# Closing block of a Winograd-form MLP product: three steps by token tile instead of two, two more sets of weight tiles, and the outputs' vector operations in another written order

## The chip, the cores and the metric

The kernel runs on one core of a Trainium2 chip. The metric is the time of one execution in device microseconds (us); a kernel's time is the median of its timed runs. The profile comes from one further execution with the hardware profiler. TensorE (PE) multiplies matrices, VectorE (DVE), ScalarE (ACT) and GpSimd (POOL) do the elementwise work, and SyncE (SP) issues the transfers (DMA).

## The reference, cut to what matters

One decoder layer for 512 tokens of width 1024 in fp32: a gated mixer of attention and convolution, then a squared-ReLU MLP, each with an RMSNorm before and after it. The change lies in the last part, the product with `w_ff2` and what follows it:

```python
f = jnp.square(jax.nn.relu(rms_norm(x, g_pre) @ w_ff1)) @ w_ff2   # (512 x 4096) @ (4096 x 1024)
x = x + rms_norm(f, g_post)          # x + f * rsqrt(mean(f*f) + eps) * g_post
```

## The kernel before, in words

**Precision.** Each fp32 operand is split in two parts, `hi` (a rounded copy, written by ScalarE) and `lo` (the rest, a subtraction on VectorE: lines 729 and 730 in `split`). `mm3` (lines 89 to 91) makes one product out of three matmuls: hi by hi, hi by lo, lo by hi. All matmuls of the stage concerned have 512 columns.

**The second MLP product** takes 16 steps `p`, each over 256 of the 4096 hidden units. A step is a 2 by 2 block product (two halves of the tokens, two halves of the 1024 columns), done in the Winograd form with seven products instead of eight. Three of the seven are summed over all steps in a first sweep, which runs together with the first MLP product. Then follows the second sweep, in which the change lies: four products `n` = 0 to 3 for two token tiles `t` = 0, 1. Each of the eight pairs (n, t) has a PSUM bank of its own, `bcc[n][t]`, that sums over p. A step of the second sweep is therefore 4 x 2 x 3 = 24 matmuls.

**Operands of a step** (`second_operands`). Four transfers of 256 KB bring quarters of `w_ff2`: one goes to tag `whi`, three to tag `raw`, which has six buffers, enough for two steps. The stationary operand `l` (split of `f1[p]`, 128x1024) has four buffers. The moving operand is a pair of weight tiles, `yh` and `yl`, each with four slices n. Tag `sw` has four buffers, that is two sets, so the split of step p into its weight tiles has to wait until the matmuls of step p - 2 have read theirs. Slice 1 is the split of a difference `t1` (line 774), the others are splits of the transferred quarters.

**Closing block.** Steps 1 to 13 go one after the other. The last TAIL = 2 steps are taken together: for t = 0 and then 1, for n = 0 to 3, the products of both steps are made, and thereby bank (n, t) is complete. What is left is VectorE's: combine the banks with the sums `e`, `g`, `h` of the first sweep into output tiles `o_[t + 2]` (from n = 0 and 1) and `o_[t]` (from n = 2 and 3), each in two column halves. `post` then takes the squares on ScalarE (line 650), the scale of the rows on GpSimd (`v_o`, line 652, and `r_o`, line 148), multiplies each half by the gain in place (line 834), and `finish` multiplies by the row scale, adds the residual `x1` (line 827) and issues the output transfer (line 828). The multiplication in place may only start when ScalarE has read the half. One of the additions to `e` is on GpSimd (line 852).

**Order of the queues.** The framework's scheduler settles each engine's order at compile time: by the order in the program, among the instructions that its own timing takes to be ready. On the chip every queue runs in that order. So the written order isn't always the order of the queue.

Of the kernel before, what the change touches and what calls it, by code (L numbers as in the profile page):

```python
# [12 lines left out]
F32R = mybir.dt.float32r  # L13
BF16 = mybir.dt.bfloat16
I32 = mybir.dt.int32
AF = mybir.ActivationFunctionType
ALU = mybir.AluOpType
# [33 lines left out]
LOOK = 2  # L51
BRIDGE = 4
SPLIT = 2 * P
TAIL = 2
LN0, LN1, LN2 = 0, 2, 3


# [1 line left out]
def decoder_block(ctx: ExitStack, tc: tile.TileContext, a: dict, out: bass.AP):  # L59
# [18 lines left out]
    def stile(name, dt=F32):  # L78
        return spool.tile([P, 512], dt, tag="s", name=name, bufs=6)

    def junk(name, n):
        return spool.tile([P, 1024], BF16, tag="s", name=name, bufs=6)[:, :n]
# [14 lines left out]
    def rtile(name, n=512):  # L97
        return stage.tile([P, 512], F32, tag="raw", name=f"raw_{name}", bufs=NRAW)[:, :n]
# [28 lines left out]
    def stat(name, n=1, tag="stat", bufs=8):  # L127
        return const.tile([P, n], F32, tag=tag, name=name, bufs=bufs)
# [17 lines left out]
    def rstd_of(v, name, n=1):  # L146
        r = stat(name, n)
        pool.tensor_tensor(r, v, mhalf if n == 1 else mhalf.broadcast_to([P, n]), ALU.pow)
        return r
# [57 lines left out]
    with ExitStack() as s1:  # L207
# [89 lines left out]
        def products(t, ab):  # L297
            for k in range(KD):
                zmm(t, k, ab)
# [220 lines left out]
    def wtile(name, dt=F32):  # L520
        return r3.tile([P, 2, 512], dt, tag="w", name=name, bufs=14)
# [124 lines left out]
    def square_sums(src, name, jk=None):  # L646

        ss = stat(f"ss_{name}", 2)
        for hf in range(2):
            act.activation(junk(f"j_{name}{hf}", 512) if jk is None else jk[:, hf, :], src[hf], AF.Square, scale=1.0 / 32.0, accum_out=ss[:, hf:hf + 1])  # L650
        v = stat(f"v_{name}")
        pool.tensor_scalar(v, ss[:, 0:1], ss[:, 1:2], EPS, ALU.add, ALU.add)
        return rstd_of(v, f"r_{name}")
# [74 lines left out]
    def split(hi, lo, src):  # L728
        act.copy(hi, src)  # L729
        dve.tensor_tensor(lo, src, f32(hi), ALU.subtract)  # L730
# [29 lines left out]
    def first_sweep(p, ops):  # L760
        left, w = ops
        for n, (bank, l) in enumerate(zip(acc, left)):
            products(bank, l, [x[:, n, :] for x in w], p == 0, p == NP - 1)

    def second_operands(p):

        b12, b11, b21, b22 = (quarter(2 * p + r, c, *t) for r, c, *t in (
            (0, 1, "whi", NSPLIT), (0, 0), (1, 0), (1, 1)))
        t1 = stage.tile([P, 512], F32, tag="wlo", name=f"t1{p}", bufs=NSPLIT)
        l = htile(f"l{p}")  # L770
        w = [r3.tile([P, 4, 512], F32R, tag="sw", name=f"y{x}{p}", bufs=4) for x in "hl"]
        split(l[:, 0:2, :], l[:, 2:4, :], f1[p])
        split(w[0][:, 0, :], w[1][:, 0, :], b11)
        dve.tensor_tensor(t1, b12, b11, ALU.subtract)
        for n, src in ((1, t1), (2, b21), (3, b22)):
            split(w[0][:, n, :], w[1][:, n, :], src)
        return l, w


# [2 lines left out]
    def second_products(p, ops, which, toks=(0, 1)):  # L782
        l, w = ops
        for n in which:
            r, c = LEFT[n]
            products(bcc[n], [l[:, r, half[c]], l[:, 2 + r, half[c]]], [x[:, n, :] for x in w], p == 0, p == NP - 1, toks)

    ops = {}
    for p in range(NP):
# [29 lines left out]
        second_products(p, second_operands(p), range(4))  # L819

    o_ = [wtile(f"o{t}") for t in range(NT)]

    def finish(t, r):
        for c, n in ((0, 512), (512, 512)) if t != 1 else ((0, 512), (512, 256), (768, 256)):
            hf, c1 = divmod(c, 512)
            piece = o_[t][:, hf, c1:c1 + n]
            dve.scalar_tensor_tensor(piece, piece, r, x1[t][hf][:, c1:c1 + n], ALU.mult, ALU.add)  # L827
            sp.dma_start(out[t * P:(t + 1) * P, c:c + n], piece)

    def post(t):  # L830
        src = [o_[t][:, hf, :] for hf in range(2)]
        r = square_sums(src, f"o{t}")
        for hf in range(2):
            dve.tensor_tensor(src[hf], src[hf], gout[:, hf * 512:(hf + 1) * 512], ALU.mult)  # L834
        finish(t, r)

    last = [(p, second_operands(p)) for p in range(NP - TAIL, NP)]
    for t in range(2):
        v = stile(f"v{t}")
        for n in (0, 1, 2, 3):  # L840
            for p, x in last:
                second_products(p, x, (n,), (t,))
            bank = bcc[n][t]
            if n == 0:
                act.copy(v, bank)
                dve.tensor_tensor(o_[t + 2][:, 0, :], v, h[:, t, :], ALU.add)
            elif n == 1:
                dve.tensor_tensor(g[:, t, :], g[:, t, :], bank, ALU.add)
                dve.tensor_tensor(e[:, t, :], e[:, t, :], bank, ALU.add)  # L849
                dve.tensor_tensor(o_[t + 2][:, 1, :], g[:, t, :], v, ALU.add)  # L850
                post(t + 2)
                pool.tensor_tensor(e[:, t, :], e[:, t, :], v, ALU.add)  # L852
            elif n == 2:
                dve.tensor_tensor(o_[t][:, 0, :], v, bank, ALU.add)
            else:
                dve.tensor_tensor(o_[t][:, 1, :], e[:, t, :], bank, ALU.add)
                post(t)


def _layout(i):  # L860
# [58 lines left out]
```

## Time and profile before

| what | value |
|---|---|
| median of 3 runs | 820.9 us (820.53 to 821.85) |
| profiled execution: its time | 821.58 us |
| its span, first to last instruction | 819.8 us |
| TensorE busy | 789.4 us, 96% of the span |
| VectorE busy | 631.7 us, 77% |
| mean granted TensorE clock | 0.985 of full |

The profiled execution took 1.78 us more than its span and 0.68 us more than the median. Times of single instructions are counted from the start of the span. A matmul's start-to-start distance in the stage concerned is 0.227 us; its shown duration of 0.39 us overlaps the next one.

### The profile page before, as it was taken

The page shows a single profiled execution, that of the slowest core. Times are in us where ns is not written, and L with a number is a line of the kernel's source. Part 1 is how long each engine was busy: PE and PEld are TensorE (multiplying, and loading weights), DVE is VectorE, ACT ScalarE, POOL GpSimd, SP SyncE. Part 2 cuts the span into 40 slices and gives each one's busy share as a digit, 9 for nine tenths or more (in the row PEclk, how much of TensorE's full clock was granted, in tenths as well). Part 3 has the DMA queues.
Part 4 walks back from the last instruction along what each step waited for, and adds up shares of the span by engine and source line. Part 5 has one row for each costly group of instructions (what it writes and reads, how often), then busy time and mean ns, then how long its engine had stood idle before and what let it go on. Part 6 is the DMA issues. An engine that isn't in the chain of part 4 may idle for free. (4 is left out here: it accounts for less than half of the span.)

```text
span 819.8 us, 11002 instructions
## 1 busy us (share of the span) xinstructions
PE 789.4 (96%) x3786; PEld 662.7 (81%) x3786; DVE 631.7 (77%) x1046; ACT 419.7 (51%) x792; POOL 215.6 (26%) x203
## 2 busy tenths in 40 slices
PE   8989999999999999899999999999999999999991
PEld 8977888888887888687877898888888888788881
DVE  5689999999999996587563538676766666798777
ACT  7566876876763323366442314444444344556642
POOL 4244334333534545647640110000000000000003
PEclk9999999999999999899999999999999999999996
DMA  8412121122112223235551014444433434565422
GB/s 269 137 42 91 52 81 53 45 88 71 65 65 90 97 97 113 93 134 171 172 191 39 17 36 154 142 167 142 162 133 129 155 128 146 179 214 204 167 69 102
DMA packets 54344, 96.36 MB, mean 118 GB/s; under 512 B 6288, under 2 KB 11280, under 8 KB 54288
## 3 DMA queue, kind: packets, MB, share of 16 engines
q1 hardware_dynamic: 53856, 94.09, 34.3%
q0 software_dynamic: 432, 1.57, 0.6%
q8 instruction: 30, 0.49, 0.3%
q14 instruction: 26, 0.21, 0.1%
HBM read 93.54 MB, written 2.10 MB: 117 GB/s over the span
## 5 line engine op out<-in xcount | busy, mean ns | idle before, releaser
L562 DVE SCALAR_TENSOR_TENSOR cv<-u,convw,cv 128x512 f32<-128x512 f32 x232 | 161.9, 747 | 0.2
L90 PE MATMUL pf<-h2l,whi_f 128*128 128x512 f32 (+1 forms) x256 | 96.2, 376 | 0.0
L89 PE MATMUL pf<-h2h,whi_f 128*128 128x512 f32 (+1 forms) x256 | 96.2, 376 | 0.0
L91 PE MATMUL pf<-h2h,wlo_f 128*128 128x512 f32 (+1 forms) x256 | 96.0, 376 | 0.0
L115 DVE TENSOR_TENSOR wlo_f<-raw_f,whi_f 128x512 fp32r<-128x512 f32 x60 | 41.1, 691 | 61.1 <-ACT whi_f L114 58.8
L852 POOL TENSOR_TENSOR e<-e,v 128x512 f32<-128x512 f32 x2 | 3.2, 1594 | 321.5 <-DVE e L849 321.5
L114 ACT CAST whi_f<-raw_f 128x512 fp32r<-128x512 f32 x60 | 36.9, 621 | 81.4 <-DMA raw_f<-in_w_ff 42.7
L115 POOL TENSOR_TENSOR wlo_gt<-raw_gt,whi_gt 128x512 fp32r<-128x512 f32 x32 | 43.9, 1373 | 50.5 <-ACT whi_gt L114 50.5
L89 PEld LDWEIGHTS pf<-h2h,whi_f 128*128 128x128 f32 x256 | 48.2, 188 | 8.8
L90 PEld LDWEIGHTS pf<-h2l,whi_f 128*128 128x128 f32 x256 | 48.2, 188 | 8.7
L91 PEld LDWEIGHTS pf<-h2h,wlo_f 128*128 128x128 f32 x256 | 48.2, 188 | 8.7
L89 PE MATMUL pg<-hTh,whi_gt 128*128 128x512 f32 x128 | 51.9, 405 | 0.0
L90 PE MATMUL pg<-hTl,whi_gt 128*128 128x512 f32 x128 | 50.8, 397 | 0.0
L91 PE MATMUL pg<-hTh,wlo_gt 128*128 128x512 f32 x128 | 50.7, 396 | 0.0
L89 PE MATMUL p<-yh,l 128*128 128x512 f32 x128 | 49.7, 390 | 0.0
L90 PE MATMUL p<-yl,l 128*128 128x512 f32 x128 | 49.7, 389 | 0.0
L91 PE MATMUL p<-yh,l 128*128 128x512 f32 x128 | 49.5, 389 | 0.0
L729 ACT CAST yh<-f 128x512 fp32r<-128x512 f32 x48 | 28.1, 619 | 32.8 <-PE p L90 25.2
L730 DVE TENSOR_TENSOR yl<-f,yh 128x512 fp32r<-128x512 f32 x48 | 31.7, 686 | 12.9 <-ACT yh L729 12.9
L114 ACT CAST whi_gt<-raw_gt 128x512 fp32r<-128x512 f32 x32 | 19.8, 618 | 41.3 <-PE pg L90 38.4
L729 ACT CAST xh<-t 128x512 fp32r<-128x512 f32 x48 | 29.8, 621 | 19.5 <-DVE t L754 19.5
L730 DVE TENSOR_TENSOR xl<-t,xh 128x512 fp32r<-128x512 f32 x48 | 31.6, 686 | 0.0
(314 smaller groups left out, 2279.8 us busy)
## 6 DMA issues: line engine op xcount, KB each, us to landing
f<-in_w_ff SPq DMA_DIRECT2D x128, 256.0 KB, 3.0
raw_f<-in_w_ff SPq DMA_DIRECT2D x64, 256.0 KB, 3.1
raw_gt<-in_w_zm SPq DMA_DIRECT2D x32, 256.0 KB, 2.5
raw_gb<-in_w_zm SPq DMA_DIRECT2D x16, 256.0 KB, 2.6
raw_ga<-in_w_zm SPq DMA_DIRECT2D x16, 256.0 KB, 2.6
raw_wo<-in_w_o SPq DMA_DIRECT2D x16, 256.0 KB, 2.6
raw_pw<-in_w_pw SPq DMA_DIRECT2D x16, 256.0 KB, 2.9
raw_wout<-in_w_out SPq DMA_DIRECT2D x16, 256.0 KB, 2.7
```

The source lines that it names most:

```text
L89: pe.matmul(o, lhsT=lh, rhs=rh, start=first, stop=False)
L90: pe.matmul(o, lhsT=lh, rhs=rl, start=False, stop=False)
L91: return pe.matmul(o, lhsT=ll, rhs=rh, start=False, stop=last)
L114: recent[act] = act.copy(hi, raw)
L115: recent[e] = e.tensor_tensor(lo, raw, f32(hi), ALU.subtract)
L562: dve.scalar_tensor_tensor(co[j] if tap == CW - 1 else acc[j], src, convw[:, i, tap:tap + 1], acc[j], ALU.mult, ALU.add)
L729: act.copy(hi, src)
L730: dve.tensor_tensor(lo, src, f32(hi), ALU.subtract)
L852: pool.tensor_tensor(e[:, t, :], e[:, t, :], v, ALU.add)
```

## The change

The closing block takes three steps together instead of two (p = 13, 14, 15). Two further sets of weight tiles come from the pool of tag `w`, whose tiles for the first MLP product's results are free by then: steps 6, 9 and 12 use set 0 and step 14 uses set 1; the other steps go on alternating over the two sets of tag `sw`. So the last three steps have three sets.

In the closing block the operations on the outputs are written in another order. A half of an output tile is now added up, squared and at once multiplied by the gain into a tile of its own (tag `raw`), no longer in place; the row scale is asked for after the second half, and `finish` of an output tile is written one or two banks later. The sum `u` = bank 1 + `v` serves both `o_[t + 2]` and `e`; with that, GpSimd's addition to `e` goes, and the additions of a bank to `g` and to `e` become additions of `u`. VectorE has 29 operations on the outputs on either side.

```diff
-TAIL = 2
+TAIL = 3
+THIRD = {6: 0, 9: 0, 12: 0, 14: 1}
...
+    spare = {}
+
+    def right_tiles(p):
+
+
+        if p in THIRD:
+            n = THIRD[p]
+            if n not in spare:
+                spare[n] = [[wtile(f"y{x}{n}{i}", F32R) for i in range(2)] for x in "hl"]
+            return [(lambda i, v=v: v[i // 2][:, i % 2, :]) for v in spare[n]]
+        return [(lambda i, v=v: v[:, i, :]) for v in (r3.tile([P, 4, 512], F32R, tag="sw", name=f"y{x}{p}", bufs=4) for x in "hl")]
+
...
-        w = [r3.tile([P, 4, 512], F32R, tag="sw", name=f"y{x}{p}", bufs=4) for x in "hl"]
+        w = right_tiles(p)
         split(l[:, 0:2, :], l[:, 2:4, :], f1[p])
-        split(w[0][:, 0, :], w[1][:, 0, :], b11)
+        split(w[0](0), w[1](0), b11)
         dve.tensor_tensor(t1, b12, b11, ALU.subtract)
         for n, src in ((1, t1), (2, b21), (3, b22)):
-            split(w[0][:, n, :], w[1][:, n, :], src)
+            split(w[0](n), w[1](n), src)
         return l, w
...
     o_ = [wtile(f"o{t}") for t in range(NT)]
+    scaled, ss_ = {}, [stat(f"ss_o{t}", 2) for t in range(NT)]
+
+    def half_row(t, hf, x, y):
+
+        o = o_[t][:, hf, :]
+        dve.tensor_tensor(o, x, y, ALU.add)
+        act.activation(junk(f"j_o{t}{hf}", 512), o, AF.Square, scale=1.0 / 32.0, accum_out=ss_[t][:, hf:hf + 1])
+        scaled[t, hf] = rtile(f"og{t}{hf}")
+        dve.tensor_tensor(scaled[t, hf], o, gout[:, hf * 512:(hf + 1) * 512], ALU.mult)
+
+    def scale_of(t):
+        v = stat(f"v_o{t}")
+        pool.tensor_scalar(v, ss_[t][:, 0:1], ss_[t][:, 1:2], EPS, ALU.add, ALU.add)
+        return rstd_of(v, f"r_o{t}")
 
     def finish(t, r):
         for c, n in ((0, 512), (512, 512)) if t != 1 else ((0, 512), (512, 256), (768, 256)):
             hf, c1 = divmod(c, 512)
-            piece = o_[t][:, hf, c1:c1 + n]
+            piece = scaled[t, hf][:, c1:c1 + n]
             dve.scalar_tensor_tensor(piece, piece, r, x1[t][hf][:, c1:c1 + n], ALU.mult, ALU.add)
             sp.dma_start(out[t * P:(t + 1) * P, c:c + n], piece)
 
-    def post(t):
-        src = [o_[t][:, hf, :] for hf in range(2)]
-        r = square_sums(src, f"o{t}")
-        for hf in range(2):
-            dve.tensor_tensor(src[hf], src[hf], gout[:, hf * 512:(hf + 1) * 512], ALU.mult)
-        finish(t, r)
-
     last = [(p, second_operands(p)) for p in range(NP - TAIL, NP)]
+    scales = {}
     for t in range(2):
-        v = stile(f"v{t}")
+        v, u = stile(f"v{t}"), stile(f"u{t}")
         for n in (0, 1, 2, 3):
             for p, x in last:
                 second_products(p, x, (n,), (t,))
             bank = bcc[n][t]
             if n == 0:
                 act.copy(v, bank)
-                dve.tensor_tensor(o_[t + 2][:, 0, :], v, h[:, t, :], ALU.add)
+                half_row(t + 2, 0, bank, h[:, t, :])
+                if t:
+                    finish(0, scales[0])
             elif n == 1:
-                dve.tensor_tensor(g[:, t, :], g[:, t, :], bank, ALU.add)
-                dve.tensor_tensor(e[:, t, :], e[:, t, :], bank, ALU.add)
-                dve.tensor_tensor(o_[t + 2][:, 1, :], g[:, t, :], v, ALU.add)
-                post(t + 2)
-                pool.tensor_tensor(e[:, t, :], e[:, t, :], v, ALU.add)
+                dve.tensor_tensor(u, bank, v, ALU.add)
+                half_row(t + 2, 1, u, g[:, t, :])
+                scales[t + 2] = scale_of(t + 2)
+                dve.tensor_tensor(e[:, t, :], e[:, t, :], u, ALU.add)
             elif n == 2:
-                dve.tensor_tensor(o_[t][:, 0, :], v, bank, ALU.add)
+                half_row(t, 0, bank, v)
+                finish(t + 2, scales[t + 2])
             else:
-                dve.tensor_tensor(o_[t][:, 1, :], e[:, t, :], bank, ALU.add)
-                post(t)
+                half_row(t, 1, bank, e[:, t, :])
+                scales[t] = scale_of(t)
+    finish(1, scales[1])
```

## Rows read from the trace of the kernel before

**Rows 1.** Page, part 1: busy us, share of the span and instructions of each engine.

```profile
PE 789.4 (96%) x3786; PEld 662.7 (81%) x3786; DVE 631.7 (77%) x1046; ACT 419.7 (51%) x792; POOL 215.6 (26%) x203
```

**Rows 2.** Busy time by stretch: length, each engine (instructions), granted clock, DMA share, GB/s.

```profile
738.50:776.00 37.50, 37.50 (x167) 31.07 (x166) 30.60 (x43) 21.44 (x35) 0.00 (x0) 1.00 0.57 196
...
795.20:803.30 8.10, 8.10 (x36) 6.39 (x35) 8.10 (x13) 2.94 (x9) 2.80 (x3) 1.00 0.15 59
803.30:819.80 16.50, 0.04 (x1) 0.00 (x0) 11.85 (x18) 3.32 (x9) 5.40 (x7) 0.58 0.26 99
```

**Rows 3.** Chain that ended last, in order of time: start us, us, what.

```profile
791.86 0.24 PE p L90
...
792.12 0.63 ACT yh L729
...
816.30 0.40 DVE o L827
```

**Rows 4.** Timeline of PE: start us, duration us, engine, line, operation, out<-in, form, count.

```profile
786.71 0.39 PE L89 MATMUL p<-yh,l 128*128 128x512 f32 x1
...
802.95 0.39 PE L91 MATMUL p<-yh,l 128*128 128x512 f32 x1
```

**Rows 5.** Timeline of ACT; in brackets the idle time before and its releaser.

```profile
792.12 0.62 ACT L729 CAST yh<-f 128x512 fp32r<-128x512 f32 x1 [3.25 <-PE p L90]
...
812.86 0.63 ACT L650 ACTIVATE j_o<-o 128x512 bf16<-128x512 f32 x1 [1.80 <-DVE o L856]
813.39 0.19 ACT L650 ACTIVATION_READ_ACCUMULATOR j_o<-o 128x1 f32 x1
```

**Rows 6.** Timeline of DVE, one step of the second sweep (12, up to 13).

```profile
776.46 0.69 DVE L730 TENSOR_TENSOR yl<-f,yh 128x512 fp32r<-128x512 f32 x1 [1.10 <-ACT yh L729]
...
778.97 1.23 DVE L730 TENSOR_TENSOR l<-f,l 128x1024 fp32r<-128x1024 f32 x1
780.12 0.69 DVE L774 TENSOR_TENSOR t<-f,f 128x512 f32<-128x512 f32 x1
781.90 0.69 DVE L730 TENSOR_TENSOR yl<-f,yh 128x512 fp32r<-128x512 f32 x1 [1.10 <-ACT yh L729]
```

**Rows 7.** Timeline of DVE, from the last step's splits to the end.

```profile
792.78 0.69 DVE L730 TENSOR_TENSOR yl<-f,yh 128x512 fp32r<-128x512 f32 x1 [2.94 <-ACT yh L729]
...
795.19 0.68 DVE L846 TENSOR_TENSOR o<-v,h 128x512 f32<-128x512 f32 x1
...
797.59 1.79 DVE L834 TENSOR_TENSOR o<-o,g_out 128x512 f32<-128x512 f32 x1
799.30 0.68 DVE L854 TENSOR_TENSOR o<-v,p 128x512 f32<-128x512 f32 x1
799.90 0.68 DVE L834 TENSOR_TENSOR o<-o,g_out 128x512 f32<-128x512 f32 x1
800.50 1.40 DVE L827 SCALAR_TENSOR_TENSOR o<-o,r_o,x 128x512 f32<-128x512 f32 x2
...
812.09 0.67 DVE L856 TENSOR_TENSOR o<-e,p 128x512 f32<-128x512 f32 x1
...
815.15 1.54 DVE L827 SCALAR_TENSOR_TENSOR o<-o,r_o,x 128x512 f32<-128x512 f32 x3 [0.85 <-POOL r_o L148]
```

**Rows 8.** Timeline of POOL in the closing block.

```profile
797.22 1.61 POOL L852 TENSOR_TENSOR e<-e,v 128x512 f32<-128x512 f32 x1 [318.75 <-DVE e L849]
...
799.63 0.56 POOL L148 TENSOR_TENSOR r_o<-v_o,mhalf 128x1 f32<-128x1 f32 x1
...
813.68 0.80 POOL L652 TENSOR_SCALAR v_o<-ss_o 128x1 f32<-128x1 f32 x1 [3.22 <-ACT j_o L650]
```

**Rows 9.** Line 725, quarters of `w_ff2` issued between 738 and 785 us.

```profile
DMA to landing us min/median/max: 2.5/3.0/4.7
```

**Rows 10.** Busy time by stretch, columns as in the second group; the clock is third last.

```profile
710.00:715.00 5.00, 4.13 (x19) 3.12 (x18) 5.00 (x9) 4.99 (x9) 0.00 (x0) 1.00 0.65 213
...
806.00:807.00 1.00, 0.00 (x0) 0.00 (x0) 1.00 (x3) 0.13 (x1) 0.00 (x0) 0.50 0.64 250
```

More of the change, by code (lines that the diff above doesn't have):

```diff
@@ L785, in second_products @@
             r, c = LEFT[n]
-            products(bcc[n], [l[:, r, half[c]], l[:, 2 + r, half[c]]], [x[:, n, :] for x in w], p == 0, p == NP - 1, toks)
+            products(bcc[n], [l[:, r, half[c]], l[:, 2 + r, half[c]]], [x(n) for x in w], p == 0, p == NP - 1, toks)
     ops = {}
```

## Prediction

> **What bounds the kernel now.** I start from the busy shares: TensorE is busy for 96% of the span [rows 1], so a change can only win in what little is left. The busy times by stretch say where that is. From 738.5 to 776 us TensorE is busy without a gap, and it still is from 795.2 to 803.3, but in the last 16.5 us it has no work, while VectorE is busy for 11.85 of them [rows 2]. The chain of waits says since when VectorE sets the end: TensorE is in the chain up to 792.1 us; there ScalarE's rounding of the last step's weights (`yh`) follows, and from then on VectorE's instructions, broken by short pieces of ScalarE and GpSimd, up to 816.7 [rows 3]. What ScalarE waited for at 792.12 was TensorE [rows 5]: step 15 fills the set of weight tiles that step 13 has just finished reading. VectorE comes to step 15's first `yl` at 792.78, having idled 2.94 us, and to the first output operation at 795.19 [rows 7]. By then TensorE has only 8 us of matmuls left; the six banks still open close within them, and VectorE falls behind: it comes to the last addition at 812.09. From that addition on, a fixed chain runs: squares on ScalarE at 812.86, the row scale on GpSimd from 813.68, the last three output pieces at 815.15 [rows 5, 7, 8], and the transfer until 819.8. That is 819.8 - 812.09 = 7.71 us, of which 3.06 lie between the addition and the first piece.
>
> TensorE's own end can hardly move. The last 72 matmuls (three steps) start at 786.71, and the last one starts at 802.95 [rows 4]: 16.24 us for 71 distances, 0.229 each, while full rate here is 0.2267 (a step of 24 takes 5.44 us, as the distance of 776.46 and 781.90 in [rows 6] also says). So at most 0.15 us is lost there. The gain has to come out of the 16.5 us behind TensorE.
>
> **The change part by part.**
>
> *Three steps in the closing block.* The same 72 matmuls, in another order: a bank now closes every 9 matmuls, 2.04 us, beginning at 786.71 + 2.04 + about 0.2 for the matmul's own length = 788.96, and the eighth at 803.24. Before, a bank closed every 1.36 us from 793.6 on. VectorE's output work can start some 6 us earlier, if its operands are done by then.
>
> *Are the operands there in time?* The closing block needs the first slice of step 15 six matmuls after 786.71: `yh` at 788.07, `yl` at 788.30. Before, `yl` was ready at 792.78 + 0.69 = 793.47. So 5.17 us have to be won, just under one step, and that is what the further sets permit: with three sets in turn from step 6 on, a step's split waits for the step three back, 5.44 us earlier. VectorE must also be quick enough. One step holds it for 5.44 us, of which it waits 1.10 [rows 6]; without the wait 4.34. The transfers allow about the same: a `raw` buffer is free after a step's first `yl` (0.69), the next quarter lands 3.0 later [rows 9], `t1` (0.60) follows: 4.3. So each step from 6 on gains up to 1.1 us, and after five steps, by step 11, the lead of one step is full. Step 13's first `yl` then starts at 781.90 - 5.44 = 776.46. Step 14 has a set of its own and follows at 780.8; step 15 at 785.2, first `yl` ready at 785.9. In the worse order, in which step 15's `l` (its buffer is free when step 11's matmuls end, 792.12 - 2 x 5.44 = 781.24) stands ahead of step 14's splits, step 14 starts at 781.24 + 1.23 for ScalarE's part (taken as long as VectorE's of the same 1024 columns, 778.97) + 1.15 for VectorE's + 0.60 for `t1` = 784.2 and step 15 at 786.6, ready at 787.3. Both are ahead of 788.30, by 2.4 and 1.0 us. The cost for TensorE is zero, hidden by this margin; without it each microsecond late costs one. VectorE is done with the operands between 787.6 and 789.0.
>
> *The output operations.* Their number on VectorE doesn't change, 29. Each of the simple ones takes 0.60 us start to start (four from 795.19 to 797.59), two pieces of `finish` 1.40 [rows 7]. GpSimd's additions to `e` go, and something more goes with them: the multiplication at 797.59 took 1.79 us, where that at 799.90 took 0.68, and GpSimd's addition ran from 797.22 to 798.83 [rows 7, 8]. The second token tile shows the same pattern, so VectorE gets back twice 1.1 us. Multiplying into a separate tile removes the wait for ScalarE's squares; before, the scheduler had put the next bank's addition (line 854, 799.30) in that place, so this gives order and little time. The scaled halves take `raw` buffers that no transfer needs any more; the two that come round again were sent out more than 7 us before.
>
> *Sum, bank by bank* (start of the first operation; bank closing in brackets), VectorE at 0.60 and 1.40: t = 0: n0 788.96 (788.96), n1 791.0 (791.0), four operations to 793.4; n2 793.4 (793.0), half a row and `finish(2)` to 796.0; n3 796.0 (795.1) to 797.2. t = 1: n0 797.2 (797.1) to 798.4; `finish(0)` waits for its scale, 796.0 + 3.06 = 799.06, to 800.46; n1 800.46 (799.2) to 802.86; n2 802.86 (801.2) to 804.06; `finish(3)` at its scale, 801.06 + 3.06 = 804.12, to 805.52; n3, the last addition, at 805.52 (803.2). Before, it was at 812.09. Gain 6.57 us. With the 7.71 us behind it the span is 813.2, and the profiled execution 821.58 - 6.6 = 815.0; it had stood 0.68 above the median, so I take the median's 820.9 - 6.6 = **814.3 us**.
>
> *Bounds.* The last addition can't come before bank (3, 1) closes: 803.24, a gain of 8.85, 812.05 us. From the other side, no lead at all: 5.17 us of the gain are lost, 819.5 us.
>
> **The rivals.**
>
> *1. Another queue order, faster.* The written order puts `finish(3)` ahead of the last addition. The scheduler has reordered here before (line 854 stands between two of line 834 [rows 7]). If it draws the last addition ahead, that starts at 804.06, and `finish(3)` lies in the shadow of the last scale: gain 8.0, 812.9 us. For it speaks that the scale comes only at 804.1; against it, that VectorE would idle only 0.06 us in the written order.
>
> *2. VectorE held up by GpSimd's small operations.* The 1.79 us of [rows 7] show that a multiplication can wait for GpSimd. Four pairs of small operations remain, some 0.56 and 0.80 long [rows 8]. If each pair held VectorE for 0.56 us, 2.2 us would be lost: 816.5. Against it stands the multiplication at 799.90, which took 0.68 although GpSimd's `r_o` ran from 799.63 to 800.19. The Trainium skill, "SBUF — State Buffer", section "Who interferes with whom", says that a VectorE instruction with two SBUF inputs and a GpSimd instruction that reads SBUF exclude each other for a whole instruction. For the large addition the trace agrees (1.79 us); for the 128x1 operations the row at 799.90 does not.
>
> *3. No lead, no change.* If the steps from 6 on gain nothing (VectorE's queue held by a `t1` whose quarter lands late, say), step 15 comes at 792.78 as now; TensorE stands still for 5.17 us in the middle of the closing block, and all banks close that much later: 819.5 us. Against it stand the 1.10 us of waiting in each step that would have to persist though its cause is gone.
>
> *4. No lead, and a lower clock: slower.* The place is the same pause at 788 us. After TensorE's end the granted clock is 0.50 at 806 us, the lower of its two levels (1.2 instead of 2.4 GHz), 2.7 us after the last matmul's end; a pause of 0.87 us within 710 to 715 left it at 1.00 [rows 10]. A pause of 5 us could thus leave some of the 66 remaining matmuls at half rate, 0.227 us more each, at most 15 us: 819.5 to 834.5. It is slower than before from the seventh such matmul on, measurably (0.2%, 1.6 us, about what a measurement of this kernel can tell from no change) from the fourteenth. The Trainium skill, "TensorE: Matmul & The Clock Gate", section "HAM oscillation — how this bites in real kernels", says that pauses for data throttle the clock and that work then goes on slowly at first; no row here shows matmuls after such a pause.
>
> **How the numbers follow.** Forecast 0.66, rival 1 0.14, rival 2 0.05, rival 3 0.10, rival 4 0.05. In rival 3 a partly built lead is as likely as none; it ends between 814.3 and 819.5, so of its 0.10 I give 0.03 to faster and 0.07 to same. Faster: 0.66 + 0.14 + 0.05 + 0.03 = 0.88; same 0.07; slower 0.05. The range goes from the bound of the early side, 812.0, over rivals 1 and 2 to 817.5, which also takes in a lead that is short by 3 us; outside it are what is left of rival 3 and rival 4. The likeliest case alone: 813 to 816.
>
> **What would show it.** In the profile after: step 13's first `yl` near 776.5 and step 15's before 788.3; TensorE without a pause up to 803; the first output operation near 789; no VectorE multiplication above 0.8 us; the last addition near 805.5; some 10 us from TensorE's end to the end of the span instead of 16.5. The prediction is wrong if TensorE pauses around 788, if the queue of VectorE holds output operations ahead of step 15's splits, or if the last addition comes later than 808.

## The result, and the profile after

The change makes the kernel faster: 816.46 us (median of 4 runs, 814.52 to 817.37) beside 820.71 us for the kernel before (4 runs, 820.40 to 821.85), a ratio of 0.9931 with the interval 0.9908 to 0.9954. The gain is 4.25 us, where 6.6 were forecast; 816.46 lies inside the range of 812.0 to 817.5, but just outside the 813 to 816 that the prediction gave for its likeliest case. The profiled execution took 816.91 us with a span of 815.1 us, where the prediction's sum gave 815.0 and 813.2.

The page's busy shares (columns as in [rows 1]) hardly move:

```profile
PE 791.0 (97%) x3786; PEld 664.7 (82%) x3786; DVE 627.9 (77%) x1046; ACT 420.3 (52%) x792; POOL 211.7 (26%) x201
```

The stretches do, which is why the stretch and not the share is to be read. Busy time by stretch of the kernel after, columns as in [rows 2]:

```profile
738.50:776.00 37.50, 37.50 (x168) 31.03 (x167) 34.47 (x50) 25.35 (x40) 0.00 (x0) 1.00 0.68 221
796.20:804.20 8.00, 8.00 (x36) 6.35 (x34) 6.82 (x12) 2.16 (x6) 0.86 (x2) 1.00 0.35 133
804.20:815.10 10.90, 0.06 (x1) 0.00 (x0) 6.38 (x11) 1.93 (x6) 1.94 (x4) 0.67 0.26 96
```

In the first stretch VectorE now works 34.47 us instead of 30.60: it waits less for a set of weight tiles and runs ahead. In the last one it has 11 instructions left instead of 18, and that stretch is 10.9 us long instead of 16.5. TensorE has its full clock up to its end and no pause in the closing block: in its timeline the first of the 72 matmuls and the last are

```profile
787.78 0.39 PE L90 MATMUL p<-yh,l 128*128 128x512 f32 x1
...
803.87 0.39 PE L92 MATMUL p<-yh,l 128*128 128x512 f32 x1
```

16.09 us for 71 distances, 0.2267 each. VectorE's timeline of the kernel after (start, duration, engine, line, operation, out<-in, form, count; in brackets the idle time before and its releaser), as [rows 6, 7] for before:

```profile
766.65 0.69 DVE L731 TENSOR_TENSOR yl<-f,yh 128x512 fp32r<-128x512 f32 x1 [1.10 <-ACT yh L730]
...
782.97 0.69 DVE L731 TENSOR_TENSOR yl<-f,yh 128x512 fp32r<-128x512 f32 x1 [0.74 <-ACT yh L730]
...
790.64 0.69 DVE L840 TENSOR_TENSOR o<-p,h 128x512 f32<-128x512 f32 x1 [3.69 <-ACT v L866]
791.37 0.69 DVE L843 TENSOR_TENSOR raw_og<-o,g_out 128x512 f32<-128x512 f32 x1
792.06 0.69 DVE L871 TENSOR_TENSOR u<-p,v 128x512 f32<-128x512 f32 x1
792.78 0.69 DVE L840 TENSOR_TENSOR o<-u,g 128x512 f32<-128x512 f32 x1
...
795.53 0.75 DVE L854 SCALAR_TENSOR_TENSOR raw_og<-raw_og,r_o,x 128x512 f32<-128x512 f32 x1 [0.25 <-POOL r_o L149]
...
798.18 0.69 DVE L843 TENSOR_TENSOR raw_og<-o,g_out 128x512 f32<-128x512 f32 x1
799.98 0.75 DVE L854 SCALAR_TENSOR_TENSOR raw_og<-raw_og,r_o,x 128x512 f32<-128x512 f32 x1 [1.11 <-POOL r_o L149]
800.65 0.69 DVE L840 TENSOR_TENSOR o<-p,h 128x512 f32<-128x512 f32 x1
...
805.98 0.75 DVE L854 SCALAR_TENSOR_TENSOR raw_og<-raw_og,r_o,x 128x512 f32<-128x512 f32 x1 [0.25 <-POOL r_o L149]
...
807.91 0.68 DVE L840 TENSOR_TENSOR o<-p,e 128x512 f32<-128x512 f32 x1
...
810.49 1.54 DVE L854 SCALAR_TENSOR_TENSOR raw_og<-raw_og,r_o,x 128x512 f32<-128x512 f32 x3 [1.17 <-POOL r_o L149]
```

Step 11's first `yl` is at 766.65 us. The operands of step 15 start at 782.97, the output operations at 790.64, after 3.69 us in which VectorE has nothing to do. The last addition is at 807.91, the last pieces end at 810.49 + 1.54 = 812.03.

**How to compare the kernels.** The start of the closing block (its first matmul) differs by some microseconds from profile to profile, by what happens upstream (run e11 shows one part of it). So each kernel is read from there on, with three numbers: S, from the block's first matmul (with two steps: from the first of the last 72, where step 13 begins) to VectorE's first output operation; L, from that operation to the end of VectorE's last pieces; T, from the start of the last matmul to the end of the span. All come from the timelines. Before: S = 795.19 - 786.71 = 8.48, L = 816.69 - 795.19 = 21.50, T = 819.8 - 802.95 = 16.86 (span 819.81). After: S = 2.86, L = 21.39, T = 11.27. In the table, T - S - L is -13.1 with two steps and -13.0 with three (the block's 16.2 or 16.1 us less 3.1 for the last transfer), so T differs between kernels only by S and L. This is partly arithmetic; what the traces add is that the 72 matmuls take 16.1 to 16.2 us and the last transfer 3.1 in every kernel of the table. S is mainly what the block changes, L mainly what the operations and their order change.

| kernel | S | L | T | ratio to before (95%) |
|---|---|---|---|---|
| before | 8.48 | 21.50 | 16.86 | 1 |
| after | 2.86 | 21.39 | 11.27 | 0.9931 (0.9908 to 0.9954) |
| e1: block alone | 2.86 | 23.79 | 13.68 | 0.9954 (0.9939 to 0.9970) |
| e2: operations alone | 8.48 | 22.13 | 17.47 | 1.0021 (1.0006 to 1.0036) |
| e3: a set for step 14 only | 3.14 | 21.76 | 11.89 | 0.9935 (0.9920 to 0.9949) |
| e4: after, queue as written | 2.86 | 20.77 | 10.66 | 0.9938 (0.9919 to 0.9956) |
| e5: after, additions first | 2.25 | 20.43 | 9.70 | 0.9900 (0.9885 to 0.9915) |
| e7: before, addition on VectorE | 8.49 | 22.72 | 18.09 | 1.0019 (1.0006 to 1.0033) |
| e8: two steps, queue of e5 | 8.48 | 20.33 | 15.69 | 0.9985 (0.9968 to 1.0001) |
| e9: e5, splits put back | 2.24 | 20.13 | 9.38 | 0.9905 (0.9889 to 0.9920) |
| e10: before, splits put back | 8.49 | 21.50 | 16.86 | 0.9988 (0.9975 to 1.0001) |
| e11: after, once more | 2.85 | 21.38 | 11.26 | 0.9939 (0.9916 to 0.9963) |

Each ratio is to runs of the kernel before on the same chip; e6 was run once and stands below.

### The profile page after: what moved, and what is told of

It is laid out like the page before. It is cut to its first block, busy times and chain, and to the rows that moved or that the text cites. A ratio compares the mean times of both kernels' runs of the same rounds, so it can differ in the third digit from the quotient of the medians.

```text
span 815.1 us, 10990 instructions
## 1 busy us (share of the span) xinstructions
PE 791.0 (97%) x3786; PEld 664.7 (82%) x3786; DVE 627.9 (77%) x1046; ACT 420.3 (52%) x792; POOL 211.7 (26%) x201
## 3 DMA queue, kind: packets, MB, share of 16 engines
q0 software_dynamic: 432, 1.57, 0.6%
```

## The experiments

### e1 and e2: the change's two halves

e1 has the three-step block and its sets with the output operations of before (below, against before). e2 is the reverse: the kernel after with these lines taken back.

```diff
-TAIL = 2
+TAIL = 3
+THIRD = {6: 0, 9: 0, 12: 0, 14: 1}
...
-        w = [r3.tile([P, 4, 512], F32R, tag="sw", name=f"y{x}{p}", bufs=4) for x in "hl"]
+        w = right_tiles(p)
```

> The three-step closing block and its weight tiles, with the output operations as they were before (gain multiplied in place, one addition to e on GpSimd). Measure: the stretch from the start of the last matmul to the end of the span, 16.85 us before the change and 11.23 us with the whole change. Theory 1, the block is the main cause: banks close every 2.04 us and VectorE keeps up, so most of the gain is there, stretch about 12.5 us, some 4.4 us faster than before. Theory 2, the order of the output operations is the main cause and VectorE is the bound in any case: the stretch stays above 15 us, gain under 2 us.

> The new output operations alone, with the closing block of two steps and two sets of weight tiles. Theory 1 (block is the main cause): VectorE still begins its output work only after step 15's splits, at 795.2 us, and is the bound from there; it gets back the two waits of 1.1 us at GpSimd's addition and some idle time, stretch from the last matmul's start to the end about 14.5 us, gain about 2.3 us. Theory 2 (order is the main cause): stretch below 12.5 us, gain above 4 us. Theory 3 (order is worth nothing): 16.8 us, no change.

e1: 818.67 us (5 runs; before 822.14, 14 runs). e2: 823.41 us (10 runs). The block alone brings T from 16.86 to 13.68, the operations alone cost 0.6, and both together bring 5.6: the halves don't add up. S shows the block's part whole, 5.62 us in e1 as in the change; e1 loses 2.29 of it in L. VectorE's timeline of e1:

```profile
790.80 0.69 DVE L859 TENSOR_TENSOR o<-v,h 128x512 f32<-128x512 f32 x1 [3.69 <-ACT v L858]
...
795.62 0.91 DVE L847 TENSOR_TENSOR o<-o,g_out 128x512 f32<-128x512 f32 x1 [0.19 <-ACT j_o L651]
...
809.99 0.68 DVE L869 TENSOR_TENSOR o<-e,p 128x512 f32<-128x512 f32 x1
...
813.05 1.54 DVE L840 SCALAR_TENSOR_TENSOR o<-o,r_o,x 128x512 f32<-128x512 f32 x3 [0.84 <-POOL r_o L149]
```

In e1 VectorE has eight idle times of 0.19 to 0.85 in the stretch, 4.84 us in all: four for the row scale, 3.36 us, and four for ScalarE's squares, 1.48 us, which must have read a half before the multiplication in place may start; the same operations in the kernel before wait three times, 1.55 us. In e2 the new operations wait for the scale four times:

```profile
801.23 1.41 DVE L841 SCALAR_TENSOR_TENSOR raw_og<-raw_og,r_o,x 128x512 f32<-128x512 f32 x2 [0.76 <-POOL r_o L148]
...
805.07 0.75 DVE L841 SCALAR_TENSOR_TENSOR raw_og<-raw_og,r_o,x 128x512 f32<-128x512 f32 x1 [1.10 <-POOL r_o L148]
...
812.13 1.42 DVE L841 SCALAR_TENSOR_TENSOR raw_og<-raw_og,r_o,x 128x512 f32<-128x512 f32 x2 [0.84 <-POOL r_o L148]
813.46 0.68 DVE L827 TENSOR_TENSOR o<-p,e 128x512 f32<-128x512 f32 x1
...
816.04 1.54 DVE L841 SCALAR_TENSOR_TENSOR raw_og<-raw_og,r_o,x 128x512 f32<-128x512 f32 x3 [1.16 <-POOL r_o L148]
```

That is 3.86 us in the four waits. Late banks aren't the reason (and behind the last of the four no addition is left): the last matmul of e2 starts at 803.21, so at 812.13 every bank is long complete, and yet the last addition stands behind these pieces, at 813.46. e8 below puts the additions ahead and has an L of 20.33 instead of 22.13. The prediction counted 2.2 us for GpSimd's hold alone, and e2's expectation 2.3 us of gain for the operations; without the block, and in the scheduler's order, they are worth nothing.

### e3: is the lead built from step 6 on needed?

```diff
-THIRD = {6: 0, 9: 0, 12: 0, 14: 1}
+THIRD = {14: 0}
```

> The change without set 0 (steps 6, 9 and 12 go back to the two alternating sets); only step 14 has a set of its own, so no step before 14 can get a lead. Theory A, a set for step 14 is enough: step 15 then takes the set of step 12, which is free when the closing block begins, its first yl is ready about 1.4 us later, just when the seventh matmul wants it: TensorE pauses 0.3 us at most, the stretch from the last matmul to the end stays within 0.7 us of 11.2 us. Theory B, as the prediction put it, the lead built from step 6 on is needed: TensorE pauses up to 5.2 us in the closing block and the time goes back to 819 to 821 us.

817.05 us (4 runs), not to be told from the change in the time; T is 11.89, 0.6 more than with the change, and TensorE doesn't pause. VectorE's timeline, from the last operands to the outputs:

```profile
788.03 1.29 DVE L731 TENSOR_TENSOR yl<-f,yh 128x512 fp32r<-128x512 f32 x2
...
790.43 0.69 DVE L840 TENSOR_TENSOR o<-p,h 128x512 f32<-128x512 f32 x1
```

A set for step 14 is enough, but only just: step 15's first `yl` is ready at 788.03 + 0.69 = 788.72, and the block, which begins at 787.29, wants it 1.59 us later, at 788.88. With this set the two old sets go to steps 12 and 15 and to step 13, so step 15's split waits for step 12's matmuls, which end as the block begins, and not for step 13's, which lie in the block. What the set for steps 6, 9 and 12 adds is the margin (5.7 us instead of 0.16) and that VectorE is done with operands at 786.9 instead of 790.4. Of the 0.6 us of T, 0.28 are S, since the first addition now stands right behind the last split; the rest is L, in which the scheduler settled another order for the second token tile.

### e4: the queue as written

The scheduler had put pieces of `finish(0)` ahead of an addition whose bank was long closed (799.98 ahead of 800.65 above). e4 chains every VectorE operation of the outputs to the one before it:

```diff
+    def vec(op, *args):
+        with ExitStack() as behind:
+            if queue[0] is not None:
+                behind.enter_context(tc.issue_after(queue[0].ins))
+            queue[0] = op(*args)
...
-        dve.tensor_tensor(o, x, y, ALU.add)
+        vec(dve.tensor_tensor, o, x, y, ALU.add)
```

> The change with VectorE's queue in the closing block held to the written order. With the change the scheduler put finish(0) ahead of the next token tile's first addition and finish(3) between the multiplications, VectorE idled 1.11 us there, and the last addition started 4.04 us after the last matmul's start where the sum had 2.57. Theory 1, the scheduler's order is the reason: last addition about 2.6 to 3.0 us after the last matmul's start, stretch to the end 9.8 to 10.2 us, about 1.2 us faster than the change. Theory 2, the reason is longer dependent steps (0.70 instead of 0.60 us) and the wait for ScalarE's copy of the first bank: nothing gained, 11.2 us.

817.59 us (4 runs), not to be told from the change in the time, but T is 10.66 instead of 11.27. VectorE's timeline:

```profile
801.68 0.69 DVE L844 TENSOR_TENSOR o<-p,h 128x512 f32<-128x512 f32 x1 [0.54 <-ACT v L875]
...
809.65 0.68 DVE L844 TENSOR_TENSOR o<-p,e 128x512 f32<-128x512 f32 x1
...
812.22 1.54 DVE L844 SCALAR_TENSOR_TENSOR raw_og<-raw_og,r_o,x 128x512 f32<-128x512 f32 x3 [1.16 <-POOL r_o L149]
```

A T of 10.66 lies between the two theories (9.8 to 10.2, and 11.2). The wait of 1.11 is gone, one of 0.54 is left, for ScalarE's copy of the same bank. In this execution the block began at 790.13, 2.35 us later than in the profiled one of the change, which is more than the gain in T (run e11 comes back to it).

### e5 and e8: additions first, with three steps and with two

e5 keeps e4's chain, writes ScalarE's copy of a bank behind VectorE's addition from it, puts additions ahead of pieces, and the last addition ahead of `finish(3)`. e8 is the same on the block of two steps with its two sets.

```diff
             if n == 0:
+                half_row(t + 2, 0, bank, h[:, t, :])
                 act.copy(v, bank)
-                half_row(t + 2, 0, bank, h[:, t, :])
                 if t:
                     finish(0, scales[0])
...
                 half_row(t, 0, bank, v)
-                finish(t + 2, scales[t + 2])
+                if t == 0:
+                    finish(2, scales[2], (0,))
             else:
                 half_row(t, 1, bank, e[:, t, :])
                 scales[t] = scale_of(t)
+                finish(t + 2, scales[t + 2], (0, 1) if t else (1,))
```

> The change with VectorE's queue held to a written order in which both additions of an output tile stand ahead of the pieces of the tile before it, and the last addition ahead of finish(3); ScalarE's copy of a bank stands behind VectorE's addition from it. Theory: what limits the stretch behind TensorE is the place of the last addition in VectorE's queue. With 0.72 us for a step that depends on the one before and 0.60 otherwise, the last addition starts 1.2 us after the last matmul's start (4.04 with the change), the last pieces at 3.9 (6.62), the stretch to the end is 8.5 us instead of 11.27: 2.8 us faster than the change, 1.0% faster than before. Rival: VectorE's sheer amount of work limits, no order helps: 10.5 us or more.

> The closing block of two steps, as before, with the new output operations in the order of the run in which the last addition stands first. The new operations alone, in the scheduler's order, gave 17.47 us behind the last matmul (16.86 before). Theory 1: there VectorE lost by waiting for row scales that stood at the head of its queue (3.9 us idle); held to this order it works without a break from 795.2 us on, 26 operations, last pieces 9 us after the last matmul's start, stretch 13.7 us. Theory 2: the operations themselves are slower and the order is not the reason: 17 us or more.

e5: 815.29 us (5 runs; before 822.73, 20 runs), the lowest T up to here, 9.70, between the 8.5 of the theory and the 10.5 of its rival. e8: 821.28 us (10 runs), in the time not to be told from before; its T of 15.69 lies between the two theories (13.7, and 17 or more). The two have the same L, 20.43 and 20.33, and differ in S by 6.23 and in T by 5.99. So with this order of the queue on either side, the three-step block is worth its earlier start and nothing else. VectorE's timeline of e5:

```profile
792.38 0.69 DVE L844 TENSOR_TENSOR o<-p,h 128x512 f32<-128x512 f32 x1 [3.07 <-PE p L92]
...
807.77 0.68 DVE L844 TENSOR_TENSOR o<-p,e 128x512 f32<-128x512 f32 x1
...
809.10 1.41 DVE L844 SCALAR_TENSOR_TENSOR raw_og<-raw_og,r_o,x 128x512 f32<-128x512 f32 x2
811.27 1.54 DVE L844 SCALAR_TENSOR_TENSOR raw_og<-raw_og,r_o,x 128x512 f32<-128x512 f32 x3 [0.76 <-POOL r_o L149]
```

The first addition now starts as its bank closes (released by TensorE, 2.25 us after the block's first matmul). The last addition begins 807.77 - 806.23 = 1.54 us after the last matmul's start (the change: 4.04). Two edits are at work here: of the 1.57 us of T that e5 wins over the change, 0.61 are S, which is the copy's new place, and 0.96 are L, which is mainly the order. But from the last addition to the last pieces it is 3.50 us instead of 2.58: the pieces of `finish(3)`, put into that gap to fill it, make the row scale late. GpSimd's timeline of e5:

```profile
809.37 1.22 POOL L856 TENSOR_SCALAR v_o<-ss_o 128x1 f32<-128x1 f32 x1 [2.03 <-ACT j_o L850]
```

In the kernel after, where VectorE was idle beside it, GpSimd's timeline has 0.30 us for this operation:

```profile
809.50 0.30 POOL L847 TENSOR_SCALAR v_o<-ss_o 128x1 f32<-128x1 f32 x1 [3.56 <-ACT j_o L841]
```

And e8's queue, first at `u` and then at its end:

```profile
797.43 0.69 DVE L831 TENSOR_TENSOR u<-p,v 128x512 f32<-128x512 f32 x1 [0.60 <-ACT v L865]
...
814.21 1.54 DVE L831 SCALAR_TENSOR_TENSOR raw_og<-raw_og,r_o,x 128x512 f32<-128x512 f32 x3 [0.76 <-POOL r_o L148]
```

### e6: step 15's operands late on purpose

Rivals 3 and 4 hang on what a pause in the block would do. Here ScalarE writes slice 0 of step 15's `yh` 16 times more, with the same values, ahead of the split; nothing is left out. TensorE's order in the block is held.

```diff
+        for _ in range(16 if p == NP - 1 else 0):
+            act.copy(w[0](0), b11)
```

> The change with step 15's weights made late on purpose: ScalarE writes the first slice 16 times more than needed (the same values), and TensorE's order in the closing block is held, so TensorE must pause there, by 4 to 5 us. It gives the price of a missing lead. As the prediction's rival 3 has it: the pause is added once, the matmuls after it run 0.227 us apart, the last matmul starts 4 to 5 us later, stretch from it to the end 11.2 us. As rival 4 has it: the granted clock falls to half during the pause and matmuls after it start 0.43 us apart, each 0.2 us more; some 8 to 16 of them, 2 to 3 us on top, 6 to 8 us in all.

823.47 us (one run), beside 822.73 for the median of before on that chip. Busy time by stretch of e6:

```profile
787.00:790.00 3.00, 0.20 (x1) 0.00 (x0) 0.00 (x0) 2.85 (x5) 0.00 (x0) 1.00 0.00 0
790.00:793.30 3.30, 0.02 (x1) 0.02 (x1) 0.04 (x1) 3.09 (x5) 0.00 (x0) 0.66 0.00 0
793.30:797.60 4.30, 4.30 (x10) 3.09 (x11) 2.04 (x3) 1.31 (x3) 0.00 (x0) 0.50 0.00 0
797.60:803.00 5.40, 5.40 (x25) 4.47 (x24) 4.10 (x7) 1.45 (x4) 1.08 (x2) 0.97 0.00 0
```

TensorE stops after six matmuls and goes on at 793.28, 6.47 us after the sixth began. The granted clock is 0.50 by then (1.2 instead of 2.4 GHz), and ten matmuls start in 4.3 us; then it is back. The block takes 24.77 us instead of 16.09: 6.24 for the pause and 2.4 for the low clock. T stays at 11.25. So a pause costs its length and, at this length, 2.4 us more: rival 4's mechanism exists, at the low end of its 0 to 15 us, and what keeps the change from it is the early operands. The Trainium skill, "TensorE: Matmul & The Clock Gate", section "HAM oscillation — how this bites in real kernels", has matmuls run slowly after a pause for data; the trace agrees, with distances of 0.43 instead of 0.2267 us.

### e7: GpSimd's addition moved to VectorE, in the kernel before

```diff
-                pool.tensor_tensor(e[:, t, :], e[:, t, :], v, ALU.add)
+                dve.tensor_tensor(e[:, t, :], e[:, t, :], v, ALU.add)
```

> The kernel before with one edit: the addition to e of line 852 on VectorE instead of GpSimd. Theory 1: the two multiplications of 1.79 and 1.75 us wait for GpSimd's addition; without it each takes 0.68, VectorE gets back 2.2 us and pays twice 0.60: stretch from the last matmul's start to the end 15.9 us instead of 16.86, 1.0 us faster. Theory 2: the long multiplications have another reason: they stay near 1.8 us and the stretch grows to 18.0 us.

823.71 us (10 runs), 1.0019 of before: slightly slower. VectorE's timeline of e7:

```profile
797.74 0.69 DVE L834 TENSOR_TENSOR o<-o,g_out 128x512 f32<-128x512 f32 x1
799.27 1.42 DVE L827 SCALAR_TENSOR_TENSOR o<-o,r_o,x 128x512 f32<-128x512 f32 x2 [0.84 <-POOL r_o L148]
...
815.32 1.54 DVE L827 SCALAR_TENSOR_TENSOR o<-o,r_o,x 128x512 f32<-128x512 f32 x3 [0.84 <-POOL r_o L148]
```

The multiplications are back at 0.69 (1.79 in [rows 7]), so it was GpSimd's addition that held them. But the scheduler then draws `finish` up to the multiplication, and VectorE waits 0.76 to 0.84 us for the row scale four times, 3.3 us, where [rows 7] have no wait before the pieces at 800.50. The hold had been hiding GpSimd's scale: the first theory has the mechanism right, and T comes out as in the second, 18.09.

### e9, e10 and e11: where the block's late start comes from

In the profiles of e4 and e5 the block began at 790.13, 2.35 us later than in the first profile of the kernel after. e11 is the change once more; e9 is e5, and e10 the kernel before, with one upstream edit: on ScalarE, the last two slices of step 0's split go behind the first sweep's last split.

```diff
-        act.copy(hi, src)
+        recent["split"] = act.copy(hi, src)
...
             with ExitStack() as behind:
+                if p == 0 and n > 1:
+                    behind.enter_context(tc.issue_after(last_first.ins))
                 split(w[0](n), w[1](n), src)
...
+    last_first = recent["split"]
     second = second_operands(0)
```

> The run with the last addition first, and one edit far ahead of it: the third and fourth split of step 0's weights stand behind the last split of the first sweep in ScalarE's queue; with that, step 1's first split, which waits for a transfer, also moves behind. In the traces so far TensorE pauses near 711 us because the first sweep's last splits stand behind splits that wait for a transfer: the distance of two matmuls was 1.3 us in most traces, and 2.3 and 2.4 us in two, and after these two 8 matmuls ran 0.43 us apart and the closing block began at 790.1 instead of 786.7 to 787.9 us. Theory 1, this pause is a main source of the scatter between executions: distance below 1.0 us, no matmul at 0.43 us after it, median 1 to 2 us below that of the run without the edit on the same chip, ratio to before about 0.988. Theory 2, the scatter comes from the start of the program alone: no change in median or scatter.

> The kernel before with that edit of ScalarE's queue alone. Theory 1: TensorE's pause near 711 us shrinks from 1.26 to below 1.0 us, 0.3 to 1 us faster than before, ratio about 0.999. Theory 2: 1.000.

> The change itself once more, on the chip of these runs, for a direct comparison and a second trace. If the stretch behind TensorE is set by the queues' order and not by chance, it is 11.2 to 11.3 us again; the start of the closing block may differ by a microsecond or more from 787.78. Ratio to before 0.993.

e11: 818.97 us (6 runs, 816.27 to 821.22; before 823.72, 17 runs); its block began at 791.25. e9: 816.12 us (5 runs, 814.75 to 816.64). e10: 822.71 us (12 runs, 820.45 to 825.52; before 822.33 to 827.00), no clear difference. How late a profile lies ahead of the pause, VectorE's timelines of before, after and e11 show, one line each:

```profile
707.58 0.69 DVE L702 TENSOR_TENSOR f<-pf,rl 128x512 f32<-128x512 f32 x1 [1.09 <-ACT rl L699]
708.54 0.69 DVE L703 TENSOR_TENSOR f<-pf,rl 128x512 f32<-128x512 f32 x1 [1.08 <-ACT rl L700]
709.38 0.69 DVE L703 TENSOR_TENSOR f<-pf,rl 128x512 f32<-128x512 f32 x1 [1.08 <-ACT rl L700]
```

This is the same instruction, and up to 738 us every engine's instructions stand, by their names, in the same order in the three traces. So 0.96 of the 1.07 us by which the block of the kernel after begins later than before, and 1.80 of the 4.54 us of e11, are there already, and the order of the queues doesn't make them. ScalarE's timeline of e11:

```profile
712.48 0.62 ACT L730 CAST yh<-f 128x512 fp32r<-128x512 f32 x1 [1.38 <-DMA f<-in_w_ff]
```

This rounding waits for a transfer, and the last `xh` of the first sweep, which TensorE needs next, stands behind it. TensorE's timeline, and then busy time by stretch, of e11:

```profile
714.71 1.11 PE L90 MATMUL p<-xh 128*128 128x512 f32 x2 [1.99 <-ACT xh L730]
```

```profile
713.00:715.00 2.00, 0.29 (x1) 0.29 (x2) 1.43 (x3) 2.00 (x5) 0.00 (x0) 0.97 0.82 264
715.00:718.40 3.40, 3.40 (x9) 2.66 (x9) 3.40 (x6) 3.11 (x5) 0.00 (x0) 0.52 0.27 98
718.40:724.00 5.60, 5.60 (x26) 4.60 (x26) 4.06 (x7) 3.18 (x4) 0.00 (x0) 1.00 0.17 47
```

A distance of 2.37 us between two matmuls, and the clock is 0.52 for 3.4 us. e4 (2.31) and e5 (2.40) show the same, each with eight matmuls 0.43 us apart. In the profiles in which this distance was 1.26 to 1.45 (before, after, e1, e2, e3, e6, e7, e8) the clock stayed at 1.00 here. By 737 us e4, e5 and e11 are 2.7 to 2.8 us further behind the kernel before than ahead of the pause, the kernel after only 0.1. The long pause stands in three of the seven profiles with three steps and in none of the four with two (e9 and e10 left out); why its transfer lands late, no run shows. With the splits put back the pause is shorter, in TensorE's timeline of e9:

```profile
712.56 0.73 PE L90 MATMUL p<-xh 128*128 128x512 f32 x2 [0.77 <-ACT xh L730]
```

1.16 us from the matmul before, no low clock, and the block begins at 787.50; e10 has 1.16 too. But the first theory wanted less than 1.0 us and a ratio near 0.988, and e9's 0.9905 can't be told from the 0.9900 of e5, which has no such edit. The runs of e9 scatter over 1.9 us, those of e11 over 5.0 and those of e5 over 4.2; but e10 scatters over 5.1 and before over 4.7, so that the edit narrows the scatter is not shown. Nor is it shown for each run that the long pause sets e11's slower ones apart. That e9's L and T are 0.3 us below e5's comes from GpSimd's last two operations: `v_o` took 0.64 us instead of 1.22, and `r_o` 0.84 instead of 0.56.

## Why the prediction was right, point by point

- **The bound.** Right: VectorE's queue behind the block sets the end. e4 and e5 change only the order of what stands behind the banks, the block keeps its 16.1 us, and T moves by 0.6 and 1.6 us.
- **The operands.** Right in effect, with an unneeded step. Step 15's first `yl` came at 782.97, where the sum had 785.2, and was ready 5.7 us before the block needed it (783.66, against 787.78 + 1.59 = 789.37); there was no pause. The lead was built "from step 6 on" as the sum had it: step 11's first `yl` came at 766.65, 21.13 us ahead of the block, where the kernel before has it at 771.02, one step ahead of the 776.46 of [rows 6] and 15.69 ahead of the same 72 matmuls. That is the 5.44 of one step. But it wasn't needed to avoid the pause: e3 has enough, by 0.16 us, with one set for step 14, as what counts is only which step's tiles step 15 takes over (step 11's in the change, step 12's in e3). The price put on a lead that fails was right in its first part, each microsecond late costs one (e6), and rival 4's low clock comes on top.
- **The sum of the output operations** is the term that was mis-sized. It had the last addition 18.81 us after the block's start; it came at 20.13, 1.32 later. The first 0.61 us (S 2.86 instead of 2.25) came from ScalarE's copy, which the first addition waited for, and was made up by `u` at 792.06, 4.28 us after the block's start as in the sum (4.29). From there on, VectorE idled 1.61 us where the sum had 0.72, because of the 1.11 us before `finish(0)` at 799.98, which the scheduler had put ahead of the addition at 800.65: that is 0.89. The other 0.44 are in the steps themselves: 0.36 of it are three that read the result of the one just before and start 0.72 us after it (792.06 to 792.78), not 0.60. e4 shows the first part: in written order T falls by 0.6. The sum had a sign for being wrong, a last addition later than 808; 807.91 stays 0.09 us below it, and in e11, the same kernel, it is at 811.37. Counted from the block's start, the two profiles agree (20.13 and 20.12 us), and that would have been the better sign.
- **The chain behind the last addition** was 7.23 us instead of 7.71, since `v_o` took 0.30 us instead of the 0.80 of [rows 8].
- **The block's own start** was 787.78 instead of 786.71. Of these 1.07 us, 0.96 are there at 708.54, ahead of any instruction that the change moves (see e11); kernels with two steps began between 785.65 and 786.97, those with three between 785.68 and 791.25. Together: 1.07 + 1.32 - 0.48 = 1.91 us, which is the span's 815.14 less the 813.23 of the sum.
- **GpSimd's addition** was right as a mechanism (e7), wrong as a price: taken alone it gives nothing back, since the wait for the row scale takes its place.
- **Rival 1** had the scheduler draw the last addition ahead of `finish(3)`. It did the opposite, it drew a piece of `finish(0)` ahead of an addition; ordered so by hand (e5) T fell by 1.6 us, near the 1.4 that the rival gave it, but by luck in part: 0.6 of it is the place of ScalarE's copy, about which the rival says nothing.
- **Rival 2** didn't come: no VectorE multiplication took over 0.69 us. The hold goes the other way round: `v_o` takes 0.30 us beside an idle VectorE, 0.52 at 804.78 and 1.22 in e5 beside one that works on two inputs in SBUF; in the kernel before it took 0.30 at 803.36 too, beside an addition with one input in PSUM (`g<-g,p`, 803.03). The Trainium skill, "SBUF — State Buffer", section "Who interferes with whom", lets a VectorE instruction with two SBUF inputs and a GpSimd instruction that reads SBUF exclude each other; the trace agrees for GpSimd, the later of the two, and its price falls on the row scale.

## What to carry to other kernels

When an engine's queue sets the end behind the last matmuls, ask two things apart: when its first instruction can start, and how long the queue then runs; the first is bought with buffers and a block that closes results earlier, the second with an order in which no instruction waits for a scale while a ready addition stands behind it. Don't add up what two such edits bring alone: the operations that lost 0.6 us by themselves won 2.4 once the block was there. And look at the order that the scheduler settled, not the written one; pinning it was worth 0.6 us of T here; the additions first, together with the copy behind them, 1.6 (e5 and e9, 0.9900 and 0.9905 of before, are the fastest versions tried).

## What the runs showed of the hardware that was not expected

- A VectorE operation of 128x512 that reads the result of the one before it starts 0.72 us after it, an independent one 0.60 to 0.61 (792.06, 792.78 and 793.39 in the kernel after), though both are shown with 0.68 to 0.69.
- GpSimd's 128x1 `v_o` took 0.30 us beside a VectorE that was idle or read one input from PSUM, and 0.51 to 1.22 beside operations with two inputs in SBUF. The neighbours alone don't fix it: beside the same two pieces, begun 0.27 us before, it took 1.22 in e5 and 0.64 in e9.
- A distance of 2.3 to 2.4 us between two matmuls was followed by eight matmuls at half the clock, in three profiles; distances of 1.16 to 1.45 us by none, in ten. A pause of 6.2 us in e6 cost 2.4 us in clock, where these eight matmuls cost 1.4 to 1.7.
